# Conditioning vector spread by TensorE instead of by DMA, at the start of a one-core SSD and attention trunk

## Chip, cores and metric

The kernel runs on one core of one Trainium2 chip. The metric is the device time of one execution in microseconds (us). Three runs of the kernel before gave a median of 1242.96 us (1242.60 to 1243.46). Every quantity of time below is in us unless it says ns.

## The reference

Two layers, each with a modulation (shift, scale, gate) that is computed from one conditioning vector `c`. Sizes: 256 tokens, width 2048, all float32.

```python
def _adaln(c, w, b):
    mod = jax.nn.silu(c) @ w + b                 # c: (1, 2048), w: (2048, 6144)
    shift, scale, gate = jnp.split(mod, 3, axis=-1)
    return shift[:, None, :], scale[:, None, :], gate[:, None, :]

for layer in range(DEPTH):                       # DEPTH = 2
    shift, scale, gate = _adaln(c, ada_w[layer], ada_b[layer])
    h = x * (1.0 + scale) + shift
    y = _ssd_mixer(h, ...) if layer < N_A_LAYERS else _dilated_mixer(h, k_sh, v_sh, ...)
    x = _layer_norm(DEEPNORM_ALPHA * x + (1.0 + gate) * y, ln_g[layer], ln_b[layer])
    if layer == N_A_LAYERS - 1:
        k_sh, v_sh = _shared_kv(x, kv_w)
```

Layer 0 is a Mamba-2 (SSD) mixer: `h @ in_w` with 10304 output columns, a short convolution, a chunked scan, an output product. Layer 1 is a dilated window attention with keys and values shared from layer 0's output. Nearly all work is in the weight products.

## The kernel before, in words

**Precision.** Each float32 weight piece (128 x 1024 values, 512 KB, tile `raw`) is split in two fp32r parts: ScalarE copies it to `whi` (`split`, L99), VectorE writes the rest `raw - whi` to `wlo` (L101), and TensorE then makes three matmuls for each block: high by high, high by low, low by high (L150 to L152 for products with the weights as stationary operand, L212 to L214 for the other orientation). The activations `h`, kept transposed with 16 blocks `kt` of 128 channels in the tile `actT`, are split in the same way into `hhi` and `hlo`.

**The modulation.** Channel block `kt` of `h` needs two numbers per channel, `scale` and `shift`. Each is a dot product of a 2048-long row of `ada_w` with silu(c). The kernel holds silu(c) in all 128 partitions (tile `cb_`, 128 x 2048). A load of 1 MB brings 128 rows of `ada_w` (tile `araw`, L288), and one VectorE instruction multiplies them by `cb_` and sums along the row (`ada_dot`, L295, a SCALAR_TENSOR_TENSOR with an accumulated output into `mod`). So each of the 16 blocks costs two loads of 1 MB and two such dot products; 96 of them in the whole program.

**The start.** `c` (8 KB in memory) is loaded with a zero stride over partitions, so that one DMA of 1 MB writes the same row in all 128 partitions (`bcast`, L63 and L67), and ScalarE applies silu to 128 x 2048 in place (L68). Behind it on the same DMA queue (SyncE, SP, issues all loads) come two `araw`, the input block `xt`, the biases `adab`, the first weight piece, two more `araw`, and then more weight pieces. SP has eight semaphores for its DMAs and uses them in turn, so the ninth load, the second weight piece, is issued when the first load, `c`, has landed.

**The step of one block**, `h_step`, called twice for each `kt`: dot product for `scale`, dot product for `shift`, the addition of the biases (`ada_bias`, L300), then on ScalarE `htmp = x * scale + shift` (L463) and `hhi` (L465), then on VectorE `hlo` (L467). For blocks 0 and 1 the program is written out by hand: after block 0, two plain float32 products start from `htmp` without a split (`plain`, L503, four matmuls of 256 columns each, which the profile counts as eight), and only the second half of their weight pieces is split (`half`, L511 and L512) for block 1. From there a list of products (`order`) is worked through piece by piece, with `h_step` calls between them; partial sums of products that cannot be finished yet are put away from PSUM to SBUF by ScalarE (`put_away`, L568). A list scheduler of the framework decides the order on each engine within these constraints, and `tc.issue_after` pins some of them.

**PSUM.** The pool `mm` has four tiles of one bank, the pool `ex` has another four, which hold the first two products (`first`) through the whole phase.

The few lines of the start that the change touches:

```python
    cb_ = cons.tile([P, D], F32, name="cb_")
    bcast(cb_, c)
    S.activation(cb_, cb_, AF.Silu)
```

## Time and profile before

| what | value |
|---|---|
| median of three runs | 1242.96 us (1242.60 to 1243.46) |
| the profiled execution, its own time | 1243.02 us |
| its span, first to last instruction | 1241.2 us |
| TensorE (PE) busy | 1216.1 us, 98% of the span, 7078 matmuls |
| weight loads of TensorE (PEld) | 1043.9 us, 84% |
| VectorE (DVE) busy | 1028.3 us, 83% |
| ScalarE (ACT) busy | 702.4 us, 57% |
| DMA read from memory | 332.47 MB, mean 270 GB/s |
| DMA in the first 155 us (five slices of the page) | 384, 421, 423, 422, 421 GB/s |

The profiled execution took 1.8 us more than its span; that part lies around the instructions. It is 0.06 us over the median of the three runs. A line of the timeline gives the start and the duration in us, the engine, the line of the program, the operation, what it writes and reads, and how many equal instructions it merges; in brackets stands the engine's idle time before it and what ended it. Matmuls overlap in the records, so the distance between two starts, and not the duration, tells the pace.

### The profile page before, as it was taken

To read this page: it belongs to the slowest core of one execution; us is meant where nothing else is said; L and a number is where in the kernel's file an instruction comes from. 1 tells how busy PE (TensorE), PEld (TensorE's weight loads), DVE (VectorE), ACT (ScalarE), POOL (GpSimd) and SP (SyncE) were. 2 spreads that over 40 slices of the span, in tenths; PEclk is the share of its full clock that TensorE was granted. 3 is DMA by queue.
4 is the path that set the end of the run, shared out by engine and by line. 5 is a ranking of instruction groups with operands and counts; after the bars stand their busy time and mean duration, and the time that the engine had idled before them with its cause. 6 is when DMAs were issued, how large, how long until landed. Compare 5 with 4: busy or idle time off the path is not lost.

```text
span 1241.2 us, 18711 instructions
## 1 busy us (share of the span) xinstructions
PE 1216.1 (98%) x7078; PEld 1043.9 (84%) x7078; DVE 1028.3 (83%) x1454; ACT 702.4 (57%) x1045; POOL 0.2 (0%) x4
## 2 busy tenths in 40 slices
PE   4999999999999999999999999999999999999997
PEld 4989988898888888888888788888888888888886
DVE  5999986999988989899768678889978867658777
ACT  3555477868597789764345544434435644444631
POOL 0000000000000000000000000000000000000000
PEclk9999999999999999999999999999999999999999
DMA  9999977687656456699998569989997774463751
GB/s 384 421 423 422 421 270 245 226 295 257 213 193 208 166 172 202 214 338 346 356 320 293 192 199 381 353 340 368 380 375 294 229 263 132 136 205 118 233 175 68
DMA packets 80587, 335.88 MB, mean 271 GB/s; under 512 B 9105, under 2 KB 9329, under 8 KB 67697
## 3 DMA queue, kind: packets, MB, share of 16 engines
q1 hardware_dynamic: 80496, 334.69, 74.9%
q8 instruction: 55, 0.90, 0.3%
q14 instruction: 36, 0.29, 0.1%
HBM read 332.47 MB, written 2.18 MB: 270 GB/s over the span
## 4 chain that ended last, share of the span: by engine, by line
PE 83%; DMA 8%; DVE 6%; ACT 2%; issue 1%; DVEq 0%; ACTq 0%; SPq 0%
PE acc L181 24%; PE acc L184 12%; PE acc L213 12%; PE acc L214 12%; PE acc L212 11%; DMA raw<-in_win 6%; DVE wlo L101 2%; PE acc L150 2%; PE acc L152 2%; PE acc L151 2%; PE py L705 1%; DVE araw L295 1%; DMA araw<-in_ada 1%; ACT whi L99 1%; PE acc L915 1%
## 5 line engine op out<-in xcount | busy, mean ns | idle before, releaser
L99 ACT ACTIVATE whi<-raw 128x1024 fp32r<-128x1024 f32 x390 | 409.5, 1058 | 355.5 <-PE acc L214 137.5
L101 DVE TENSOR_TENSOR wlo<-raw,whi 128x1024 fp32r<-128x1024 f32 x390 | 470.3, 1221 | 142.9 <-ACT whi L99 138.4
L181 PE MATMUL acc<-actT,whi 128*128 128x512 f32 x1280 | 405.3, 397 | 0.0
L184 PEld LDWEIGHTS acc<-actT,wlo 128*128 128x128 f32 x1280 | 239.4, 188 | 55.6 <-DVE wlo L101 0.4
L213 PE MATMUL acc<-wlo,actT 128*128 128x512 f32 x656 | 257.1, 392 | 0.8 <-DVE wlo L101 0.8
L212 PE MATMUL acc<-whi,actT 128*128 128x512 f32 x656 | 253.3, 394 | 0.0
L184 PE MATMUL acc<-actT,wlo 128*128 128x256 f32 x1280 | 252.9, 279 | 0.0
L295 DVE SCALAR_TENSOR_TENSOR araw<-araw,cb__72 128x2048 f32<-128x2048 f32 x96 | 219.3, 2285 | 9.9 <-DMA araw<-in_ada 9.8
L181 PEld LDWEIGHTS acc<-actT,whi 128*128 128x128 f32 x1280 | 195.9, 189 | 0.4
L214 PE MATMUL acc<-whi,actT 128*128 128x512 f32 x432 | 169.0, 391 | 0.0
L213 PEld LDWEIGHTS acc<-wlo,actT 128*128 128x128 f32 x656 | 123.2, 188 | 27.2 <-DVE wlo L101 2.1
L212 PEld LDWEIGHTS acc<-whi,actT 128*128 128x128 f32 x656 | 122.7, 188 | 24.1
L150 PE MATMUL acc<-actT,whi 128*128 128x256 f32 x376 | 106.9, 286 | 0.0
L151 PE MATMUL acc<-actT,whi 128*128 128x256 f32 x376 | 106.1, 284 | 0.0
L152 PE MATMUL acc<-actT,wlo 128*128 128x256 f32 x376 | 104.6, 285 | 0.4 <-DVE wlo L101 0.4
L214 PEld LDWEIGHTS acc<-whi,actT 128*128 128x128 f32 x432 | 81.1, 188 | 16.7
L214 PE MATMUL acc<-whi,ylo 128*128 128x512 f32 x224 | 87.5, 391 | 0.0
L150 PEld LDWEIGHTS acc<-actT,whi 128*128 128x128 f32 x376 | 72.7, 193 | 0.6
L151 PEld LDWEIGHTS acc<-actT,whi 128*128 128x128 f32 x376 | 72.7, 193 | 0.4
L152 PEld LDWEIGHTS acc<-actT,wlo 128*128 128x128 f32 x376 | 71.5, 193 | 0.7 <-DVE wlo L101 0.6
L214 PEld LDWEIGHTS acc<-whi,ylo 128*128 128x128 f32 x224 | 42.1, 188 | 8.6
L663 ACT ACTIVATE seg<-cbc,cumT 128x128 f32<-128x128 f32 x128 | 41.0, 389 | 5.1 <-DVE wlo L101 2.3
(278 smaller groups left out, 1124.2 us busy)
## 6 DMA issues: line engine op xcount, KB each, us to landing
araw<-in_ada SPq DMA_DIRECT2D x96, 1024.0 KB, 7.4
raw<-in_win SPq DMA_DIRECT2D x112, 512.0 KB, 6.7
raw<-in_wout SPq DMA_DIRECT2D x64, 512.0 KB, 5.9
raw<-in_wbin SPq DMA_DIRECT2D x64, 512.0 KB, 4.2
raw<-in_wxs SPq DMA_DIRECT2D x48, 512.0 KB, 4.6
raw<-in_wv SPq DMA_DIRECT2D x48, 512.0 KB, 6.7
raw<-in_wk SPq DMA_DIRECT2D x48, 512.0 KB, 7.6
cbc<-cumd SPq DMA_DIRECT2D x16, 512.0 KB, 5.0
```

The costliest lines, as they stand in the source:

```text
L99: copied.append(S.activation(hi, raw, AF.Copy))
L101: latest.append(V.tensor_tensor(lo, raw, hi.bitcast(F32), op=ALU.subtract))
L150: T.matmul(o, hi[:, k, c_], ahi[:, kt, :], start=first, stop=False, skip_group_check=True)
L151: T.matmul(o, hi[:, k, c_], alo[:, kt, :], start=False, stop=False, skip_group_check=True)
L152: T.matmul(o, lo[:, k, c_], ahi[:, kt, :], start=False, stop=kt == k1 - 1, skip_group_check=True)
L181: T.matmul(ps[n], hi[:, k, n * P:n * P + P], both(kt), start=kt == 0, stop=False, skip_group_check=True)
L184: T.matmul(ps[n][:, 0, :], lo[:, k, n * P:n * P + P], high(kt), start=False, stop=kt == KT - 1, skip_group_check=True)
L212: T.matmul(o, h_, hi[:, k, :], start=kt == k0, stop=False, skip_group_check=part)
L213: T.matmul(o, h_, lo[:, k, :], start=False, stop=False, skip_group_check=part)
L214: end = T.matmul(o, l_, hi[:, k, :], start=False, stop=kt == k1 - 1, skip_group_check=part)
L295: return V.scalar_tensor_tensor(raw, raw, 1.0, cb_, op0=ALU.mult, op1=ALU.mult, accum_out=mod[layer][:, ct, j:j + 1])
L663: S.activation(seg[:, hh, b, :], cbc[:, hh, b, :], AF.Relu, bias=cumT[:, b, h0 + hh:h0 + hh + 1], scale=-1.0)
```

## The change

`c` is laid out by the host as 16 rows of 128 values, with a 16 x 16 identity beside it (16 x 144 values, 9 KB). One small DMA brings it to 16 partitions, into a corner of `cb_`, and silu is applied to 16 x 128. TensorE then makes, for each row `j`, one matmul whose stationary operand is column `j` of the identity repeated 128 times and whose moving operand is the 16 x 128 block: it writes row `j` to all 128 partitions of a PSUM tile `cps` (128 x 2048, four banks, in a pool that is closed before `ex` is opened). Six matmuls of a tile of ones with itself stand ahead of these sixteen. ScalarE copies the four banks to `cb_`. The two dot products of block 0 read `cps` instead of `cb_`; the first is made as two halves of 1024 with an addition behind them. The "+1" on two of the biases (L519) moves behind the second dot product in the program.

```diff
     cb_ = cons.tile([P, D], F32, name="cb_")
-    bcast(cb_, c)
-    S.activation(cb_, cb_, AF.Silu)
+    crow = cb_[:KT, :P + KT]
+    nc.sync.dma_start(crow, c)
+    S.activation(crow[:, :P], crow[:, :P], AF.Silu)
...
-                ex = c0.enter_context(tc.tile_pool(name="ex", bufs=4, space=PSUM))
-                first = [acc_pair(ex), acc_pair(ex)]
+                cE = ExitStack()
+                ec = cE.enter_context(tc.tile_pool(name="ec", bufs=1, space=PSUM))
+                cps = ec.tile([P, D], F32, name="cps")
+                warm = mm.tile([P, 2, L], F32, name="acc")[:, 0, :P]
+                for _ in range(6):
+                    T.matmul(warm, ones, ones, start=True, stop=True)
+                for j in range(KT):
+                    T.matmul(cps[:, j * P:j * P + P], crow[:, P + j:P + j + 1].to_broadcast([KT, P]), crow[:, :P],
+                             start=True, stop=True)
+                for n in range(4):
+                    S.activation(cb_[:, 512 * n:512 * n + 512], cps[:, 512 * n:512 * n + 512], AF.Copy)
...
-                    h_step.dot = ada_dot(0, kind, kt, raw)
+                    if not kt and kind == "scale":
+                        part0 = mod[0][:, 0, 2:3]
+                        V.scalar_tensor_tensor(raw[:, :D // 2], raw[:, :D // 2], 1.0, cps[:, :D // 2], op0=ALU.mult,
+                                               op1=ALU.mult, accum_out=part0)
+                        V.scalar_tensor_tensor(raw[:, D // 2:], raw[:, D // 2:], 1.0, cps[:, D // 2:], op0=ALU.mult,
+                                               op1=ALU.mult, accum_out=scale(0, 0))
+                        V.tensor_tensor(scale(0, 0), scale(0, 0), part0, op=ALU.add)
+                    else:
+                        h_step.dot = ada_dot(0, kind, kt, raw, cps if not kt else None)
...
                     if kind == "shift":
+                        if not kt:
+                            with tc.issue_after(h_step.dot.ins):
+                                V.tensor_scalar(adab[:, :, :, 1:3], adab[:, :, :, 1:3], 1.0, None, op0=ALU.add)
...
-                V.tensor_scalar(adab[:, :, :, 1:3], adab[:, :, :, 1:3], 1.0, None, op0=ALU.add)
...
+                cE.close()
+                ex = c0.enter_context(tc.tile_pool(name="ex", bufs=4, space=PSUM))
+                first = [acc_pair(ex), acc_pair(ex)]
+                pss[-2], pss[-1] = first
```

The order of the instructions moves at three places. `DMAHW0` to `DMAHW7` are the semaphores of SP's loads, `Activation` counts ScalarE's instructions, `PE` TensorE's, `DVE` VectorE's own.

On VectorE, from the first dot product to the split of the second weight piece, there stood before (`cb__72` is `cb_`, `mod_84` holds shift, scale and gate of layer 0):

```order
L295 SCALAR_TENSOR_TENSOR araw,mod_84<-araw,cb__72 128x2048 [waits DMAHW1_49,Activation_49]
L295 SCALAR_TENSOR_TENSOR araw,mod_84<-araw,cb__72 128x2048 [waits DMAHW2_49]
L519 TENSOR_SCALAR adab<-adab 128x32x2 [waits DMAHW4_49]
L300 TENSOR_TENSOR mod_84<-mod_84,adab 128x2 [waits DVE_49]
L467 TENSOR_TENSOR actT<-htmp,actT 128x256 [waits Activation_49]
L512 TENSOR_TENSOR wlo<-raw,whi 128x512 [waits DMAHW5_49,Activation_49]
L295 SCALAR_TENSOR_TENSOR araw,mod_84<-araw,cb__72 128x2048 [waits DMAHW6_49]
L295 SCALAR_TENSOR_TENSOR araw,mod_84<-araw,cb__72 128x2048 [waits DMAHW7_49]
L300 TENSOR_TENSOR mod_84<-mod_84,adab 128x2 [waits DVE_49]
L467 TENSOR_TENSOR actT<-htmp,actT 128x256 [waits Activation_49]
L512 TENSOR_TENSOR wlo<-raw,whi 128x512 [waits DMAHW0_49,Activation_49]
```

and now:

```order
L464 SCALAR_TENSOR_TENSOR araw,mod_84<-araw,cps 128x1024 [waits DMAHW1_49,PE_49,Activation_49]
L466 SCALAR_TENSOR_TENSOR araw,mod_84<-araw,cps 128x1024
L296 SCALAR_TENSOR_TENSOR araw,mod_84<-araw,cps 128x2048 [waits DMAHW2_49]
L468 TENSOR_TENSOR mod_84<-mod_84 128x1 [waits DVE_49]
L480 TENSOR_SCALAR adab<-adab 128x32x2 [waits DMAHW4_49]
L301 TENSOR_TENSOR mod_84<-mod_84,adab 128x2 [waits DVE_49]
L488 TENSOR_TENSOR actT<-htmp,actT 128x256 [waits Activation_49]
L296 SCALAR_TENSOR_TENSOR araw,mod_84<-araw,cb__72 128x2048 [waits DMAHW6_49,DMAHW0_49]
L533 TENSOR_TENSOR wlo<-raw,whi 128x512 [waits DMAHW5_49,Activation_49]
L296 SCALAR_TENSOR_TENSOR araw,mod_84<-araw,cb__72 128x2048 [waits DMAHW7_49]
L301 TENSOR_TENSOR mod_84<-mod_84,adab 128x2 [waits DVE_49]
L488 TENSOR_TENSOR actT<-htmp,actT 128x256 [waits Activation_49]
```

The first dot product has a wait on TensorE and on ScalarE where it had one on ScalarE; the addition of the two halves is new; and the third dot product (block 1, scale) now stands ahead of the half split of the first weight piece, which stood ahead of it.

In the built program the first half's wait on `PE` is for the count 22, six and sixteen matmuls, which TensorE raises once behind the sixth and once behind the sixteenth; its wait on `Activation` is for the count 5, the silu and four copies, and the four copies raise that count once, behind the fourth.

On ScalarE the program began before with:

```order
L68 ACT_TABLE_LOAD
L68 ACTIVATE cb__72<-cb__72 128x2048 [waits DMAHW0_49]
L463 ACTIVATE htmp<-xt,mod_84 128x256 [waits DMAHW3_49,DVE_49]
L465 ACTIVATE actT<-htmp 128x256 [waits Activation_49]
L511 ACTIVATE whi<-raw 128x512 [waits DMAHW5_49]
```

and begins now with:

```order
L69 ACT_TABLE_LOAD
L69 ACTIVATE cb__72<-cb__72 16x128 [waits DMAHW0_49]
L442 ACTIVATE cb__72<-cps 128x512 [waits PE_49,Activation_49]
L442 ACTIVATE cb__72<-cps 128x512 x3
L484 ACTIVATE htmp<-xt,mod_84 128x256 [waits DMAHW3_49,DVE_49]
L486 ACTIVATE actT<-htmp 128x256 [waits Activation_49]
```

The copies of the spread rows stand between the silu and block 0's `htmp`; the first of them waits for TensorE's count 22 too, since `cb_`'s corner is what the matmuls read.

A little later on ScalarE, from the split of the third weight piece on (`s_101`, `s_103` are the places where two partial sums are put away), there stood before:

```order
L99 ACTIVATE whi<-raw 128x1024 [waits DMAHW1_49]
L99 ACTIVATE whi<-raw 128x1024 [waits DMAHW2_49]
L568 ACTIVATE s_101<-acc 128x512 [waits PE_49]
L99 ACTIVATE whi<-raw 128x1024 [waits DMAHW3_49,PE_49]
L568 ACTIVATE s_101<-acc 128x512 [waits PE_49]
L568 ACTIVATE s_103<-acc 128x512 [waits PE_49] x2
L99 ACTIVATE whi<-raw 128x1024 [waits DMAHW4_49,DVE_49]
```

and now:

```order
L100 ACTIVATE whi<-raw 128x1024 [waits DMAHW1_49]
L592 ACTIVATE s_101<-acc 128x512 [waits PE_49] x2
L100 ACTIVATE whi<-raw 128x1024 [waits DMAHW2_49]
L592 ACTIVATE s_103<-acc 128x512 [waits PE_49] x2
L100 ACTIVATE whi<-raw 128x1024 [waits DMAHW3_49]
L100 ACTIVATE whi<-raw 128x1024 [waits DMAHW4_49,DVE_49]
```

Two put-aways moved ahead of the fourth piece's copy and two ahead of the fifth's. Behind these places the order of all engines is the one before.

More of the change, by code (lines that the diff above doesn't have):

```diff
@@ L289, in ada_load, with ada_dot @@
         return raw
-    def ada_dot(layer, kind, ct, raw):
+    def ada_dot(layer, kind, ct, raw, by=None):
         j = KIND.index(kind)
         with tc.issue_after(pin[0]) if pin[0] is not None else ExitStack():
-            return V.scalar_tensor_tensor(raw, raw, 1.0, cb_, op0=ALU.mult, op1=ALU.mult,
+            return V.scalar_tensor_tensor(raw, raw, 1.0, by if by is not None else cb_, op0=ALU.mult, op1=ALU.mult,
                                    accum_out=mod[layer][:, ct, j:j + 1])
@@ L487, in trunk @@
                 source = {"dt": wdt, -2: win[0], -1: win[4], **{n: p[0] for n, p in zip(names, begun.values())}}
-                pss = {-2: first[0], -1: first[1]}
+                pss = {}
                 pieces = []
@@ L1236, in _layout @@
     return {
-        "xT": x[0].T.reshape(KT, P, L).transpose(1, 0, 2), "x": x[0], "c": c, "par": par, "cst": cst, "bias": bias,
+        "xT": x[0].T.reshape(KT, P, L).transpose(1, 0, 2), "x": x[0], "c": np.concatenate([c.reshape(KT, P), np.eye(KT, dtype=f)], 1), "par": par, "cst": cst, "bias": bias,
         "lnrow": np.stack([ln_g[0], ln_b[0], ln_g[1], ln_b[1]]),
```

## Prediction

> **What bounds the kernel now.** The first view is the table of stretches: length of the stretch, busy time of TensorE (PE) with its number of matmuls, then weight loads, VectorE (DVE), ScalarE (ACT), GpSimd, granted clock, DMA share and GB/s.
>
> ```profile
> 14.00:25.00 11.00, 9.04 (x24) 7.04 (x25) 8.44 (x11) 4.53 (x8) 0.00 (x0) 1.00 1.03 425
> 25.00:160.00 135.00, 135.00 (x920) 125.86 (x919) 125.98 (x134) 72.55 (x95) 0.00 (x0) 1.00 1.02 420
> ```
>
> From 25 to 160 us TensorE is busy for all of 135.00 us, VectorE for 126 of them, and the DMA engines are full at 420 GB/s. Three resources run side by side; the one that never pauses is TensorE. Whatever the change does at the start, it can reach the end only by moving TensorE's work behind 25 us earlier or later. So the second view is TensorE's timeline up to there, for its pace (the distance of two starts).
>
> ```profile
> 14.02 3.78 PE L503 MATMUL acc<-htmp,raw 128*128 128x256 f32 x8 [14.02 <-ACT htmp L463]
> 19.74 3.78 PE L503 MATMUL acc<-htmp,raw 128*128 128x256 f32 x8 [1.94 <-DMA raw<-in_win]
> 25.23 0.41 PE L150 MATMUL acc<-actT,whi 128*128 128x256 f32 x1
> 25.45 0.35 PE L151 MATMUL acc<-actT,whi 128*128 128x256 f32 x1
> 25.63 0.28 PE L152 MATMUL acc<-actT,wlo 128*128 128x256 f32 x1
> 25.75 0.28 PE L150 MATMUL acc<-actT,whi 128*128 128x256 f32 x1
> ```
>
> TensorE starts at 14.02, waits from 17.80 to 19.74 for a weight piece, and then runs on. Up to 25.45 a fp32r matmul of 256 columns takes 0.21 to 0.22 us, behind 25.63 it takes 0.12: a slow pace and a fast one. The first run of 3.78 us stayed slow; the unbroken run from 19.74 turned fast 5.8 us after its start.
>
> The third view is VectorE's timeline from the first dot product (L295) to the split of the piece that TensorE needs next at 42 us. Of the rows between, those are left out that only repeat a kind.
>
> ```profile
> 8.36 2.29 DVE L295 SCALAR_TENSOR_TENSOR araw<-araw,cb__72 128x2048 f32<-128x2048 f32 x1 [7.36 <-DMA araw<-in_ada]
> 10.58 0.08 DVE L295 DVE_READ_ACCUMULATOR araw<-araw,cb__72 128x1 f32 x1
> ...
> 12.95 0.19 DVE L519 TENSOR_SCALAR adab<-adab 128x64 f32<-128x64 f32 x1
> 13.17 0.16 DVE L300 TENSOR_TENSOR mod<-mod,adab 128x2 f32<-128x2 f32 x1
> 14.44 0.42 DVE L467 TENSOR_TENSOR actT<-htmp,actT 128x256 fp32r<-128x256 f32 x1 [1.11 <-ACT actT L465]
> 14.96 0.69 DVE L512 TENSOR_TENSOR wlo<-raw,whi 128x512 fp32r<-128x512 f32 x1
> 15.97 2.29 DVE L295 SCALAR_TENSOR_TENSOR araw<-araw,cb__72 128x2048 f32<-128x2048 f32 x1 [0.32 <-DMA araw<-in_ada]
> 18.48 2.29 DVE L295 SCALAR_TENSOR_TENSOR araw<-araw,cb__72 128x2048 f32<-128x2048 f32 x1 [0.20 <-DMA araw<-in_ada]
> 20.81 0.16 DVE L300 TENSOR_TENSOR mod<-mod,adab 128x2 f32<-128x2 f32 x1
> 22.09 0.43 DVE L467 TENSOR_TENSOR actT<-htmp,actT 128x256 fp32r<-128x256 f32 x1 [1.12 <-ACT actT L465]
> 23.56 2.36 DVE L101 TENSOR_TENSOR wlo<-raw,whi 128x1024 fp32r<-128x1024 f32 x2 [0.25 <-ACT whi L99]
> 26.93 1.22 DVE L101 TENSOR_TENSOR wlo<-raw,whi 128x1024 fp32r<-128x1024 f32 x1 [1.01 <-ACT whi L99]
> 34.59 1.23 DVE L101 TENSOR_TENSOR wlo<-raw,whi 128x1024 fp32r<-128x1024 f32 x1 [0.69 <-ACT whi L99]
> 35.73 0.42 DVE L467 TENSOR_TENSOR actT<-htmp,actT 128x256 fp32r<-128x256 f32 x1
> 36.07 2.28 DVE L295 SCALAR_TENSOR_TENSOR araw<-araw,cb__72 128x2048 f32<-128x2048 f32 x1
> 38.28 0.08 DVE L295 DVE_READ_ACCUMULATOR araw<-araw,cb__72 128x1 f32 x1
> 40.61 0.16 DVE L300 TENSOR_TENSOR mod<-mod,adab 128x2 f32<-128x2 f32 x1
> 40.72 1.23 DVE L101 TENSOR_TENSOR wlo<-raw,whi 128x1024 fp32r<-128x1024 f32 x1
> ```
>
> At the end of this stretch the two engines touch:
>
> ```profile
> 41.80 0.28 PE L151 MATMUL acc<-actT,whi 128*128 128x256 f32 x1
> 42.00 0.39 PE L152 MATMUL acc<-actT,wlo 128*128 128x256 f32 x1
> ```
>
> The subtraction that starts at 40.72 ends at 41.95, and TensorE's matmul with its `wlo` starts at 42.00, 0.08 later than the pace of 0.12 would have it. Here TensorE has no reserve against VectorE: if VectorE's chain from its first dot product to this subtraction ends later, TensorE and all behind it are later by that much. That chain is what I sum.
>
> **The change, part by part.** *When the first dot product can start.* The wait that ended last before it was its own load (8.36); the silu was done before. In the new order it waits for all sixteen spreading matmuls and for all four copies, as the counts 22 and 5 say; the second half of the dot has no wait of its own. So cutting it into halves starts nothing early. I sum TensorE's time, then ScalarE's.
>
> ```profile
> 0.73 0.38 SPq L63 DMA_DIRECT2D cb__72<-in_c  x1
> 0.82 0.17 DVE L84 MEMSET ones<- 128x128 f32 x1 [0.82 <-PEq L1252]
> 1145.99 1.05 PE L1055 MATMUL po<-pT,b 128*128 128x128 f32 x8
> ```
>
> The warm-up matmuls can start when `ones` is written, at about 1.05. A plain fp32 matmul shows as two rows. Eight rows of 256 columns took 3.78; less the 0.20 by which a slow row outlasts its pace (0.41 against 0.21) that is 0.45 each, and 0.22 for 128 columns (estimate). Six matmuls are 12 rows: 2.6, to 3.65. Sixteen spreading matmuls are 32 rows. At the fast pace a row of 128 columns takes 0.11 (eight rows in 1.05, less 0.16 of tail). Bounds: 32 x 0.11 = 3.5 if all are fast, 32 x 0.22 = 7.0 if all are slow. Between them the pace turns where an unbroken run is between 3.8 us (did not turn) and 5.8 us (had turned) old; from 1.05 on that is 4.85 to 6.85. I take the middle, 5.85: 10 rows slow, 22 fast, 8.25; with 0.2 for the last result, 8.45. The ends give 8.0 and 9.0, no turn at all 10.85. No row has matmuls with 16 partitions; I price them by their columns, and keep "no turn" as a rival. [...]
>
> What could be later than the warm-up is `c` itself. Its 1 MB was there at 5.84 (below); the next megabyte took until 8.36, 2.5 more. So 9 KB land at the latest at 5.84 - 2.5 = 3.3, at the earliest soon behind the issue at 1.11; silu on 128 columns takes at most the 0.42 of a copy of 256. At most 3.7, hidden by the warm-up to within 0.1.
>
> ```profile
> 5.84 1.91 ACT L68 ACTIVATE cb__72<-cb__72 128x2048 f32<-128x2048 f32 x1 [3.83 <-DMA cb__72<-in_c]
> 13.37 0.60 ACT L463 ACTIVATE htmp<-xt,mod 128x256 f32<-128x256 f32 x1 [5.62 <-DVE mod L300]
> 14.00 0.42 ACT L465 ACTIVATE actT<-htmp 128x256 fp32r<-128x256 f32 x1
> 22.48 1.99 ACT L99 ACTIVATE whi<-raw 128x1024 fp32r<-128x1024 f32 x2
> 26.80 1.55 ACT L568 ACTIVATE s<-acc 128x512 f32<-128x512 f32 x3
> ```
>
> Four copies of 512 from PSUM: three take 1.55, four 2.1. With two hops of 0.05 the first dot product starts at 8.45 + 2.1 + 0.1 = **10.65** (10.2 to 11.2; 13.05 without a turn), against 8.36. Its load, 2.5 earlier, is there at 5.9 and is no longer what ends last. Behind the waiting dot on VectorE stand all further dots and splits; behind the copies on ScalarE stands only block 0's `htmp`, which needs the dots anyway. [...]
>
> *VectorE's chain behind it, first part* (to the subtraction at 22.09). Before: 22.09 - 8.36 = 13.73. Now, start to start: two halves at the 1.14 of an equally long subtraction, 2.28; a dot product 2.22 (8.36 to 10.58; reading PSUM is priced like SBUF); the addition 0.11 (40.61 to 40.72); biases +1, 0.22; bias and the way over ScalarE to the subtraction, 1.27; subtraction 0.34 (35.73 to 36.07); the third dot 2.21; half split 0.60 (between 0.34 and 1.14); the fourth dot 2.33 (38.28 to 40.61); bias and ScalarE 1.28. Sum 12.86, so 0.87 less than before: the waits for loads at 15.97 and 18.48 go, since the loads land 2.5 earlier, and the half split has its ScalarE copy ready.
>
> *Second part* (22.09 to 40.72, 18.63). The same instructions. Before, VectorE waited on ScalarE for 0.25 + 1.01 + 0.69 = 1.95. Now two put-aways stand ahead of each of two copies: each makes VectorE wait 2 x 0.52 (from 1.55 for three) plus a copy of 1.0, less its own subtraction of 1.14: 0.9, twice, and 0.3 for the first; 2.1 in all. So 18.78.
>
> Sum: 10.65 + 12.86 + 18.78 = 42.29 against 40.72, **1.6 us later**. TensorE itself is ready sooner: its first split matmuls follow the ScalarE copy of block 1, at about 23.4, and it is fast by then, as the plain products run unbroken from 16.7. Their first twelve took 2.8 before, up to 25.75; at 0.12 they end at 24.85, 0.9 ahead. So TensorE waits some 2.5 at the place where it had no reserve. *Free of cost:* the accumulator that the warm-up takes, one of four, reused behind TensorE's own work; `ex` opening late, as `cps` is last read at about 15; the "+1", still behind the two dots; the second weight piece, issued at once and 2.5 sooner, at 17.2, when TensorE is still in the first product; 1 MB less of DMA, which only gives the loads a longer lead.
>
> The profiled execution took 1243.02 (0.06 over the median); 1243.02 + 1.6 = **1244.6**.
>
> **The rivals.** *No turn of the pace* while 16 partitions are in use, or a break between warm-up and spread: the first dot at 13.05, all else equal, 4.0 later, 1247.0, slower. For: the run from 14.02 stayed slow for 3.78 us. Against: nothing distinguishes the rows but their partitions. It decides from a first dot at 11.55 on: there the delay passes 2.5 us.
>
> *The DMA lead decides.* The chain of waits in this phase names loads:
>
> ```profile
> 61.20 11.52 DMA raw<-in_win
> 72.80 11.69 DMA raw<-in_win
> ```
>
> If the stage to 155 us were set by the full queue, 1 MB less would end it 2.5 earlier: 1240.6. Against it stands TensorE's 135.00 of 135.00. The chain runs through loads because each was issued when a buffer came free, 11.5 us before; that is a queue's length, not a shortage.
>
> *The halves work as named*, so that the first starts behind eight matmuls and beside the copies: about 6.7, and the sum is 2.0 to 2.5 earlier than before, 1240.5 to 1241.0. Against it stand the counts 22 and 5.
>
> **How the numbers follow.** The forecast has 0.62, no turn 0.20, the DMA lead 0.06, working halves 0.07, 0.05 something not listed. The forecast's own range is a first dot at 10.2 to 11.2, +1.1 to +2.1, and with 0.4 for runs among themselves 1243.7 to 1245.5. The range reaches up over the no-turn case and down below the time before: 1242.6 to 1247.3. A measurement of this kernel tells about 0.2%, 2.5 us, from no change. Slower by more has the no-turn case and 0.12 of the forecast's upper end, 0.32; faster by more, half of the two early cases, 0.06; within it, 0.62.
>
> **What would show it.** The first dot product between 10.2 and 11.2, straight behind the fourth copy, with its load long landed; no gap between warm-up and spread, and the pace turning within the spread; TensorE's longest wait behind 25 us at a `wlo` matmul near 43.5; from there the same work as before at a constant distance. I am wrong if the first dot starts before the last copy ends, if TensorE's start and not VectorE's chain sets the distance, or if the distance shrinks behind 50 us.

## The result, and the profile after

The changed kernel takes 1247.57 us (median of 18 executions, 1243.03 to 1250.50) against 1243.06 for the kernel before (18 executions, 1242.60 to 1244.53). The ratio is 1.0030, 95% interval 1.0023 to 1.0037: 3.7 us slower, 2.9 to 4.6. That is the distance of the means (1246.9 and 1243.2); the medians lie 4.5 apart. Two more measurements, below, gave 1.0026 and 1.0027. I had forecast +1.6 and a range of 1242.6 to 1247.3; the median lies 0.3 above that range, the time before plus 3.7 within it. My rival "no turn of the pace" had +4.0.

The median is not the time of any one kind of execution. Each execution lists its mean granted TensorE clock, and by it the 39 executions of the changed kernel, from the three measurements, fall into three groups (65 executions of the kernel before beside them: median 1243.13):

| mean granted clock | executions | time, median (range) |
|---|---|---|
| 0.993 to 0.995 | 10 | 1243.80 (1243.03 to 1245.01) |
| 0.999 to 1.000 | 16 | 1247.02 (1245.73 to 1248.18) |
| 0.997 to 0.998 | 13 | 1248.23 (1247.14 to 1250.50) |

The profile that came with the result is of the first group (1243.79, span 1242.0). Its table of stretches, with the columns as in the prediction:

```profile
14.00:25.00 11.00, 8.45 (x30) 6.70 (x31) 8.35 (x15) 4.49 (x8) 0.00 (x0) 0.65 1.02 421
25.00:160.00 135.00, 133.27 (x907) 124.05 (x906) 126.55 (x135) 71.83 (x96) 0.00 (x0) 1.00 1.01 416
```

TensorE now lacks 1.73 of its 135.00, where before it lacked nothing. Its clock column has 0.65 between 14 and 25: by the trace's records the granted clock was 1.00 from 4.62 to 8.04, 0.50 from there to 21.69, and 1.00 again behind it. The timeline of the start, TensorE, then ScalarE, then VectorE, and the place behind 40 us:

```profile
1.04 2.93 PE L437 MATMUL acc<-ones 128*128 128x128 f32 x12 [1.04 <-DVE ones L85]
3.90 4.16 PE L439 MATMUL cps<-cb__72 16*128 16x128 f32 x32
```

```profile
8.16 2.06 ACT L442 ACTIVATE cb__72<-cps 128x512 f32<-128x512 f32 x4 [5.42 <-PE cps L439]
```

```profile
10.26 1.22 DVE L464 SCALAR_TENSOR_TENSOR araw<-araw,cps 128x1024 f32<-128x1024 f32 x1 [9.26 <-ACT cb__72 L442]
...
41.65 1.22 DVE L102 TENSOR_TENSOR wlo<-raw,whi 128x1024 fp32r<-128x1024 f32 x1
```

```profile
42.93 0.39 PE L153 MATMUL acc<-actT,wlo 128*128 128x256 f32 x1 [1.73 <-DVE wlo L102]
```

Twelve warm-up rows, straight behind them 32 rows of the spread in 4.16 us (0.13 each on average, so most of them fast), four copies, the first dot product at 10.26, and at 41.65 the subtraction that stood at 40.72 before. TensorE waits 1.73 for it. The chain is the one I summed; in this execution it is 0.93 late at that place.

The last experiment brought a profile of the same kernel in an execution of the third group (1247.78, span 1246.0). The same places:

```profile
1.04 2.93 PE L437 MATMUL acc<-ones 128*128 128x128 f32 x12 [1.04 <-DVE ones L85]
3.90 7.19 PE L439 MATMUL cps<-cb__72 16*128 16x128 f32 x32
...
45.98 0.38 PE L153 MATMUL acc<-actT,wlo 128*128 128x256 f32 x1 [1.73 <-DVE wlo L102]
...
47.36 0.41 PE L153 MATMUL acc<-actT,wlo 128*128 128x256 f32 x1
47.58 0.41 PE L151 MATMUL acc<-actT,whi 128*128 128x256 f32 x1
```

```profile
13.29 1.22 DVE L464 SCALAR_TENSOR_TENSOR araw<-araw,cps 128x1024 f32<-128x1024 f32 x1 [12.29 <-ACT cb__72 L442]
...
44.70 1.23 DVE L102 TENSOR_TENSOR wlo<-raw,whi 128x1024 fp32r<-128x1024 f32 x1
...
136.08 1.41 DVE L590 TENSOR_TENSOR s<-acc,s 128x512 f32<-128x512 f32 x2 [0.75 <-PE acc L153]
...
160.27 1.22 DVE L102 TENSOR_TENSOR wlo<-raw,whi 128x1024 fp32r<-128x1024 f32 x1
```

The spread takes 7.19, so all of its rows are at the slow pace, 0.22. The first dot product starts at 13.29, the subtraction at 44.70, 3.98 later than before. Then something comes that the first profile doesn't have: behind its wait, from 47.15 to 50.56, TensorE runs at the slow pace again (16 rows 0.21 apart instead of 0.12, a loss of 1.5). At 136.08 VectorE waits 0.75 for an accumulator of TensorE. For a while TensorE, not VectorE, is the late one.

**Where the time comes from.** I take one VectorE instruction near the end of the stage, the subtraction that starts at 155.97 before, as a mark. It starts 0.14 later in the first profile and 4.30 later in the second. What follows the mark takes 1085.3 before, and 1085.9 and 1085.7 in these two. Over all fourteen profiles of this study it is 1084.2 to 1087.1, whatever the kernel's start was, so a single total carries about 1 us of chance from there. I compare kernels at the mark, and totals only as medians.

Between 41 and 155 us the distance does not stay constant, as I had said it would. It shrinks by 0.8 in both profiles, nearly all of it at three VectorE instructions between 96 and 107 us. The kernel before, and the changed one in the first profile, at the first of them and at the mark:

```profile
96.39 2.29 DVE L295 SCALAR_TENSOR_TENSOR araw<-araw,cb__72 128x2048 f32<-128x2048 f32 x1 [0.27 <-DMA araw<-in_ada]
...
155.97 1.22 DVE L101 TENSOR_TENSOR wlo<-raw,whi 128x1024 fp32r<-128x1024 f32 x1
```

```profile
96.92 2.29 DVE L296 SCALAR_TENSOR_TENSOR araw<-araw,cb__72 128x2048 f32<-128x2048 f32 x1
...
156.11 1.22 DVE L102 TENSOR_TENSOR wlo<-raw,whi 128x1024 fp32r<-128x1024 f32 x1
```

Before, VectorE waits 0.27 there for a load, and 0.08 and 0.07 at two instructions behind it; each wait also costs the 0.08 by which neighbouring rows overlap otherwise. After, it is later, and all three waits are gone. By 107 us the distance has fallen from 0.93 to 0.15. For the first wait the view names the load; the second comes straight behind a ScalarE copy that had waited 0.24 for a load; the third it doesn't name. So the loads were a second bound, close behind VectorE's chain. With the mark the account of the second profile closes: 3.98 at the subtraction, 3.21 behind the loads, 3.35 before VectorE's wait for TensorE, 4.30 behind it. The other 0.46 of its 4.76 lie behind the mark, in what is chance from profile to profile.

### The profile page after: what moved, and what is told of

It reads as the page before. It is cut to its first block, busy times and chain, and to the rows that moved or that the text cites. A ratio compares the mean times of both kernels' runs of the same rounds, so it can differ in the third digit from the quotient of the medians.

```text
span 1242.0 us, 18810 instructions
## 1 busy us (share of the span) xinstructions
PE 1221.3 (98%) x7122; PEld 1049.3 (84%) x7122; DVE 1027.8 (83%) x1457; ACT 701.5 (56%) x1049; POOL 0.2 (0%) x4
## 4 chain that ended last, share of the span: by engine, by line
PE 88%; DVE 7%; ACT 2%; DMA 2%; issue 1%; DVEq 0%; SPq 0%; ACTq 0%
PE acc L182 24%; PE acc L185 12%; PE acc L214 12%; PE acc L215 12%; PE acc L213 12%; PE acc L151 3%; PE acc L153 3%; PE acc L152 3%; DVE araw L296 2%; DVE wlo L102 1%; PE py L729 1%; ACT whi L100 1%; DMA raw<-in_wv 1%; PE acc L939 1%; PE aux L1053 1%
## 5 line engine op out<-in xcount | busy, mean ns | idle before, releaser
L296 DVE SCALAR_TENSOR_TENSOR araw<-araw,cb__72 128x2048 f32<-128x2048 f32 x94 | 214.8, 2285 | 0.4 <-DMA araw<-in_ada 0.4
```

Of the source, the lines that this page charges most:

```text
L296: return V.scalar_tensor_tensor(raw, raw, 1.0, by if by is not None else cb_, op0=ALU.mult, op1=ALU.mult, accum_out=mod[layer][:, ct, j:j ...
```

## The experiments

Each kernel stands beside the kernel before on the same chip. Times are medians, in brackets the 95% interval of the ratio. The columns "second dot", "subtraction" and "mark" are starts on VectorE in the profile: the dot product behind the first one (10.73 before), the subtraction at 40.72 before, and the mark at 155.97 before.

| kernel | us (before) | ratio | second dot | subtraction | mark, against before |
|---|---|---|---|---|---|
| changed (result's profile) | 1247.57 (1243.06) | 1.0030 [1.0023, 1.0037] | 12.55 | 41.65 | +0.14 |
| changed, again | 1246.69 (1243.22) | 1.0026 [1.0017, 1.0035] | 12.56 | 41.66 | +0.14 |
| changed, third | 1247.02 (1243.12) | 1.0027 [1.0016, 1.0037] | 15.58 | 44.70 | +4.30 |
| spread on 128 rows | 1243.78 (1243.22) | 1.0007 [0.9998, 1.0016] | 12.61 | 41.72 | +0.21 |
| that, with a load behind `c` | 1244.88 (1243.55) | 1.0016 [1.0007, 1.0025] | 12.82 | 42.11 | +0.60 |
| no warm-up | 1244.70 (1243.22) | 1.0014 [1.0005, 1.0023] | 14.41 | 43.32 | +1.80 |
| warm-up on 16 rows | 1246.44 (1243.55) | 1.0026 [1.0015, 1.0036] | 15.29 | 44.38 | +2.85 |
| ten warm-ups | 1247.10 (1243.43) | 1.0030 [1.0019, 1.0042] | 17.29 | 46.41 | +6.02 |
| per bank | 1244.90 (1243.55) | 1.0015 [1.0006, 1.0024] | 12.91 | 42.22 | +0.70 |
| per bank, no warm-up | 1242.64 (1243.43) | 0.9996 [0.9987, 1.0005] | 11.82 | 40.93 | -0.59 |
| fp32r, 4 x 512 | 1242.11 (1243.55) | 0.9989 [0.9981, 0.9998] | 9.55 | 38.85 | -1.40 |
| fp32r, again | 1242.22 (1243.12) | 0.9994 [0.9985, 1.0002] | 9.59 | 39.88 | -1.43 |
| fp32r, with a load behind `c` | 1243.91 (1243.43) | 1.0001 [0.9992, 1.0010] | 11.28 | 40.53 | +0.70 |

From the second dot product to the subtraction twelve of these thirteen profiles take 28.9 to 29.3, whatever came before. In the second fp32r profile (30.29) TensorE waited 1.93 for a weight piece, its granted clock between 14 and 25 us was 0.84 (1.00 in the first fp32r profile), and ScalarE's put-away waited for it; the kernel before (29.99) waited for loads and has another order there. So in these profiles the whole change acts through one number, the start of that dot product; and between the subtraction and the mark 0.8 is given back, unless loads or a fallen clock come in.

**The changed kernel again.**

> The changed kernel as it is, to see one of its longer executions. Theory A (TensorE's pace does not turn fast during the spread in most executions, since matmuls on 16 partitions do not keep the clock released): the profile shows 32 rows of the spread at 0.21 us, ending near 10.9, the first dot product near 13.1, and the time 1246.5 to 1248.5; a few executions, in which the turn falls into the spread, stay at 1243 to 1244. Theory B (the start is always as in the first profile, first dot at 10.3, and the longer executions lose their time later in the program): the spread ends near 8.1 and an idle stretch of 3 to 5 us stands somewhere behind 45 us. On theory A alone I reach about 1246.8, so a part of 1 us of the median of 1247.57 is not explained yet.

1246.69 against 1243.22, so the slowdown is no matter of one chip. Three of the 11 executions had a clock of 0.993 or 0.994 and took 1243.80 to 1244.57, the other eight 1245.88 to 1248.91. The profile was again one of the short ones (second dot at 12.56). What follows: there are two kinds of executions, and the mean clock tells them apart. What makes the longer ones long this run doesn't show, since none of them was profiled.

**Spread on 128 rows.** The host pads the 16 rows with zeros, so that the matmuls contract over 128 partitions; columns, number and place stay.

```diff
-    crow = cb_[:KT, :P + KT]
+    crow = cb_[:, :P + KT]
...
-                    T.matmul(cps[:, j * P:j * P + P], crow[:, P + j:P + j + 1].to_broadcast([KT, P]), crow[:, :P],
+                    T.matmul(cps[:, j * P:j * P + P], crow[:, P + j:P + j + 1].to_broadcast([P, P]), crow[:, :P],
```

> The same sixteen spreading matmuls, but over 128 partitions: rows 16 to 127 of c and of the identity are zeros, so the result is the same, and the load is 74 KB instead of 9 KB. Theory A: with all partitions in use the run from 1.05 on is unbroken work, the pace turns fast at the latest 7.9 us into the program in every execution, the spread ends between 7.7 and 9.4, and all executions lie at 1243 to 1245. Theory A' (zeros or few values in the array count as no activity, not the number of partitions): no difference from the kernel after, median 1247 to 1248. Theory B: no difference either.

1243.78, and all eleven executions had a clock of 0.995 to 0.997 and took at most 1246.20. I read that as an early turn in every one of them; the profile shows it for one, with a granted clock of 0.92 in the first 14 us and a spread that ends at 8.12. The 7.9 by which the turn was to come was an estimate of mine that no run shows. The spread:

```profile
3.77 4.35 PE L439 MATMUL cps<-cb__72 128*128 128x128 f32 x32
```

What follows: with the same instructions in the same place, the spread took 4.35 on 128 partitions, with a clock of 0.995 to 0.997 in all 11 executions; on 16 it took 4.16 in the first profile and 7.19 in the long one, and 10 executions of 39 had a clock of 0.993 to 0.995. The rows added are zeros, so it isn't the values. This takes back 2.9 us of the 3.5 by which the changed kernel was slower on that chip.

**No warm-up.** The six matmuls of `ones` are left out.

```diff
-                for _ in range(6):
-                    T.matmul(warm, ones, ones, start=True, stop=True)
```

> Without the six warm-up matmuls. Theory A: the spread starts at 2.8 instead of 3.9, runs slow throughout in every execution and ends at 9.8 instead of 10.95, so the first dot product comes at about 12.0; all executions lie close together at about 1.1 us below the long executions of the kernel after, 1245.5 to 1247, and none at 1243. Theory C (the warm-up does what it is named for, and the spread keeps it going): the spread is slower without it than with it in most executions and the median is above the kernel after.

1244.70, 2.0 faster than with them on the same chip, and 0.8 below the lower end of what I had expected. No execution turned early (clocks 0.999 to 1.000). In the profile the spread ran slow throughout, but it started at 2.74 instead of 3.90. TensorE's spread and VectorE's first dot product:

```profile
2.74 7.19 PE L436 MATMUL cps<-cb__72 16*128 16x128 f32 x32 [2.74 <-ACT cb__72 L69]
```

```profile
12.12 1.22 DVE L461 SCALAR_TENSOR_TENSOR araw<-araw,cps 128x1024 f32<-128x1024 f32 x1 [11.13 <-ACT cb__72 L439]
```

What follows: ahead of a spread on 16 partitions the warm-ups cost more, by the 1.16 by which they delay it, than they gain in the one execution of four in which they turn the pace. The 1.16 is not all of the 2.0: the long profile above loses 1.5 at the slow pace from 47.15 to 50.56, as other executions with warm-ups may, and about 0.7 stays unexplained (last experiment).

**Warm-up on 16 rows.**

```diff
-                    T.matmul(warm, ones, ones, start=True, stop=True)
+                    T.matmul(warm, ones[:KT], ones[:KT], start=True, stop=True)
```

> The six warm-up matmuls use 16 of the 128 partitions of the tile of ones; number, columns and place stay. Theory A (matmuls on 16 partitions never bring TensorE to its fast pace; in the changed kernel only the warm-up does, in about one execution of four): no execution has a granted clock of 0.993 or 0.994, all have 0.997 or more; the profile shows the spread of 32 rows at 0.21 to 0.22 each, 6.9 us from 3.9 on, the first dot product at about 13.0, and the median lies at 1247 to 1248. Theory B (partitions do not matter, the phase of the clock does): the profile is that of the changed kernel (spread 4.2 us, first dot at 10.3, clock 0.994), about a quarter of the executions are short ones, and the median is 1246.7.

TensorE's warm-up and spread, then VectorE's first dot product:

```profile
1.04 2.92 PE L437 MATMUL acc<-ones 16*128 16x128 f32 x12 [1.04 <-DVE ones L85]
3.77 7.03 PE L439 MATMUL cps<-cb__72 16*128 16x128 f32 x32
```

```profile
13.00 1.22 DVE L464 SCALAR_TENSOR_TENSOR araw<-araw,cps 128x1024 f32<-128x1024 f32 x1 [12.00 <-ACT cb__72 L442]
```

44 rows without a gap, ten us of them, and no turn: theory A. Six of the seven executions had a clock of 0.999 or 1.000; one showed 0.949 without being longer (1246.85), and I have no trace of it. The median, 1246.44, is 0.6 under what I had expected, since I had not yet found the 0.8 that the loads give back: +2.85 at the mark is +2.9 in the time.

**Per bank.** The rows of `c` go to another tile (`cc`, loaded later), `cps` becomes four tiles of a bank, each bank is copied behind its own four matmuls, and the dot products read the copy.

```diff
+    crow = cc[:KT, :P + KT]
...
-                cps = ec.tile([P, D], F32, name="cps")
+                cps = [ec.tile([P, 512], F32, name=f"cps{n}") for n in range(4)]
...
-                for n in range(4):
-                    S.activation(cb_[:, 512 * n:512 * n + 512], cps[:, 512 * n:512 * n + 512], AF.Copy)
+                    if j % 4 == 3:
+                        S.activation(cb_[:, 128 * j - 384:128 * j + 128], cps[j // 4], AF.Copy)
```

> The 16 rows of c lie in another tile than the one that the copies write, the PSUM tile is four tiles of a bank each, each bank is copied behind its own four matmuls, and the first dot products read the copy. Warm-ups stay. Theory C (the halves gain nothing because one tile for all four banks makes the copies wait for all 16 matmuls and the dot for all four copies): copies run beside the matmuls, the first half dot starts 0.1 behind the second copy (about 6.6 in an execution with the early turn), the second half behind the fourth (about 8.6), so the end of the first dot product lies 2.7 earlier than in the changed kernel, in the profile and in every kind of execution: median 1244.0, short executions 1241.2. Rival (something else holds the first dot product back, or the stage behind it absorbs the gain): within 0.5 us of the changed kernel's 1246.7.

ScalarE's second copy and VectorE's two halves, in an execution without the early turn:

```profile
7.72 0.60 ACT L442 ACTIVATE cb__72<-cps 128x512 f32<-128x512 f32 x1 [1.11 <-PE cps L439]
```

```profile
8.35 1.23 DVE L464 SCALAR_TENSOR_TENSOR araw<-araw,cb__72 128x1024 f32<-128x1024 f32 x1 [7.35 <-ACT cb__72 L442]
...
11.76 1.23 DVE L466 SCALAR_TENSOR_TENSOR araw<-araw,cb__72 128x1024 f32<-128x1024 f32 x1 [2.18 <-ACT cb__72 L442]
```

The first half starts behind the second copy, while TensorE still spreads, and the second dot product comes 2.67 earlier than in the long profile of the changed kernel (12.91 against 15.58). The time is 1.35 over the kernel before, where the changed kernel's three medians are 3.5 to 4.5 over: 2.1 to 3.2 less, around the 2.7; the rival (within 0.5) is out. The median is 0.9 above the 1244.0 that I had expected, and the one execution with an early turn (clock 0.993) took 1243.68, not 1241.2. What follows: the wait for all sixteen matmuls and all four copies came from the tiles, and cutting the dot product into halves gains only where the tiles are cut too. Which of the three cuts (another tile for `c`, a tile per bank, dots that read the copy) is needed the run doesn't separate.

**Per bank, no warm-up**: both edits together.

> The per-bank kernel without its six warm-up matmuls, spread still with plain matmuls on 16 rows. The spread starts with silu's end at 2.75 instead of 3.90, all slow, a bank each 1.78; fourth copy done at 10.4, second half of the first dot at 10.5 (11.76 with warm-ups). Theory (what counts is when the first dot product ends, and the stage gives back 0.8 of any delay up to 155 us): the dot ends 0.4 later than before, the time is 0.4 under the kernel before to equal. Rival (the warm-ups bring something besides the spread's pace, for instance an earlier turn behind it): no better than with warm-ups, 1244.9 against 1243.5.

VectorE's second half:

```profile
10.67 1.23 DVE L463 SCALAR_TENSOR_TENSOR araw<-araw,cb__72 128x1024 f32<-128x1024 f32 x1 [2.18 <-ACT cb__72 L439]
```

1242.64 against 1243.43; the interval of the ratio covers 1, so the total doesn't tell it from the kernel before. The mark is 0.59 earlier than before. With warm-ups the distance was +1.35, so the rival is out.

**fp32r, 4 x 512.** Tiles as in the per-bank kernel; `c` as 4 rows of 512, split in a high and a low part, two fp32r matmuls a bank.

```diff
...
+                S.activation(chi, crow, AF.Copy)
+                V.tensor_tensor(clo[:, :512], crow[:, :512], chi[:, :512].bitcast(F32), op=ALU.subtract)
+                for n in range(4):
+                    for part, c4 in enumerate((chi, clo)):
+                        T.matmul(cps[n], chi[:, 512 + n:513 + n].to_broadcast([4, P]), c4[:, :512],
+                                 start=not part, stop=bool(part))
+                    S.activation(cb_[:, 512 * n:512 * n + 512], cps[n], AF.Copy)
```

> As the per-bank kernel, but c comes as 4 rows of 512 with a 4 x 4 identity, is split into a high and a low fp32r part (ScalarE copy, VectorE subtraction), and each bank gets two fp32r matmuls of 512 columns instead of four plain ones of 128; no warm-ups. At the slow pace a row of 512 fp32r columns should take 0.42, eight rows 3.4 us, from about 3.6 to 7.2; first half dot at about 6.0, second at about 7.7. Theory (the end of the whole program follows VectorE's chain, one us for one us, also when it is earlier than before): 2.4 us less than the kernel before, 1240.8. Rival (the start of TensorE or the loads bind as soon as VectorE's chain is earlier): no better than the kernel before, 1243.2 or above, with TensorE or VectorE waiting for a load between 14 and 50 us.

1242.11 against 1243.55, 1.4 less where I had expected 2.4. Half of the missing 1.0 is lost ahead of 40 us: the second half of the dot started at 8.40 instead of 7.7, and VectorE's chain is 1.87 earlier at the subtraction (38.85), not 2.4. The other half is lost behind it, where ScalarE waits longer for weight pieces than before (7.0 between 25 and 50 us, against 4.2). Its waits there (line, what for, us in total, times, longest):

```profile
ACT whi L100 <- DMA raw<-in_win: 7.0, 3, 3.5
```

The third of these waits, before and now, and the VectorE subtraction that is held up in turn:

```profile
43.77 1.06 ACT L99 ACTIVATE whi<-raw 128x1024 fp32r<-128x1024 f32 x1 [0.96 <-DMA raw<-in_win]
```

```profile
42.93 1.06 ACT L100 ACTIVATE whi<-raw 128x1024 fp32r<-128x1024 f32 x1 [1.99 <-DMA raw<-in_win]
```

```profile
45.94 1.23 DVE L102 TENSOR_TENSOR wlo<-raw,whi 128x1024 fp32r<-128x1024 f32 x1 [0.39 <-ACT whi L100]
```

The piece is there 0.84 earlier than before, not 1.87, and at 45.94 the distance falls from 1.86 to 1.39. TensorE's granted clock between 25 and 50 us was 0.93 here (1.00 before). The one wait near it that the view puts down to TensorE (0.38, at 49.95) stands also in the second fp32r profile (0.37), where the granted clock of that stretch was 1.00, and it is made up by 51.64. What follows: with the chain out of the way the loads bind, and what is left at the mark is 1.40. The second measurement (below) finds 1.43 there, though its subtraction stood at 39.88.

**A load behind `c`**, 0.92 MB, which puts back nearly the megabyte that the change takes out; once in the kernel with the spread on 128 rows, once in the fp32r kernel.

```diff
     nc.sync.dma_start(crow, c)
+    nc.sync.dma_start(cb_[:, 256:], ada[0, 2, 0][:, 256:])
```

> The kernel with c on 128 partitions (the spread on 128 rows), with one load more of 0.92 MB right behind c, into the part of the tile that the copies overwrite later. It puts back nearly all of the megabyte that the change takes out. Theory (the lead of the loads is worth nothing): the same time as without it, 1243.8, up to 0.3 more, the first dot product still behind the copies at 10.3. Rival (the full queue sets the end of the stage up to 155 us): 0.92 MB at 400 GB/s are 2.3 us, 1246.1.

> The fp32r kernel with the load of 0.92 MB right behind c put back, as in the run on 128 rows, where it moved VectorE by nothing that the first dot product had not. Theory (loads come second: they bind only where VectorE's chain is earlier than before; in the fp32r kernel ScalarE waits 1.5, 3.5 and 2.0 us for weight pieces at 31, 37 and 43 us): here the load costs 1 to 2.3 us, and the time comes back to the kernel before, within 0.5. Rival (what keeps the fp32r kernel from its full gain is only the fall of TensorE's clock at 41 us): the same as without the load, 1.4 under the kernel before.

On 128 rows the first dot product still waits for the copies,

```profile
10.53 1.22 DVE L465 SCALAR_TENSOR_TENSOR araw<-araw,cps 128x1024 f32<-128x1024 f32 x1 [9.53 <-ACT cb__72 L443]
```

0.21 later than without the load, and the mark is 0.39 later; the rival's 2.3 is not there. The medians are 0.8 apart in their distance to before, more than the 0.3 that I had allowed, but their intervals overlap and leave it unclear. In the fp32r kernel the load costs 2.10 at the mark and 1.4 to 1.9 in the distance to before: the first dot product waits for its own rows,

```profile
8.78 1.23 DVE L465 SCALAR_TENSOR_TENSOR araw<-araw,cb__72 128x1024 f32<-128x1024 f32 x1 [4.45 <-DMA araw<-in_ada]
```

and all the gain is gone. So the rival, that only the fall of the clock keeps the fp32r kernel from its full gain, is out. What follows: the lead of the loads is worth little, 0.4 at the mark, while the first dot product is as late as in the changed kernel's first profile, and up to 2 us once it isn't.

**Ten warm-ups.**

```diff
-                for _ in range(6):
+                for _ in range(10):
                     T.matmul(warm, ones, ones, start=True, stop=True)
```

> Ten warm-up matmuls instead of six. [...] The spread starts 1.6 later, at about 5.5, so an execution that hits has its first dot product at 10.5 to 11.5, one that does not at 14.7: median 1244 to 1245. Rival B (whether the pace turns has nothing to do with the length of the warm-up): a quarter of the executions with the low mean clock, and a median near 1248.

Three of six executions had a clock of 0.992 to 0.994 (1244.83 to 1246.86), three of 0.998 or more (1247.34 to 1249.29). An execution that "hits" is one of the first kind. Half of them did, more than the quarter of the rival, and six executions can't tell. The expected median of 1244 to 1245 took it that most would, which was my estimate and is not shown; 1247.10 missed it. The profile was one without a turn, with 4.64 us of warm-up:

```profile
1.05 4.64 PE L437 MATMUL acc<-ones 128*128 128x128 f32 x20 [1.05 <-DVE ones L85]
5.61 7.19 PE L439 MATMUL cps<-cb__72 16*128 16x128 f32 x32
```

In the two short profiles of the changed kernel 2.93 us of warm-up stand ahead of a spread of 4.16 and 4.17, in its long one and in the per-bank profile the same 2.93 ahead of 7.19, and here 4.64 ahead of 7.19. So a longer warm-up doesn't by itself bring the fast pace. What decides, beside the partitions, no run here shows.

**fp32r and the changed kernel, on one chip.**

> The fp32r kernel once more, on one chip with the changed kernel. If its gain is that of the profile at 155 us (1.4 us earlier than before), the ratio is 0.9989 again, with an interval that excludes 1; if the first result was scatter between executions, the interval covers 1.

> The changed kernel once more, on the same chip. Theory: two kinds of executions. Where the warm-up turns the pace (clock 0.993 or 0.994, about a quarter) the time is 0.5 to 1 over the kernel before; in the others the profile with 16-row warm-ups gives 2.9 at 155 us, so 2.9 over the kernel before, and 1.5 more in those with a clock of 0.998 or less, where TensorE's longer wait near 45 us costs it a window of half clock. Rival: no kinds, one spread of times around 2.5 over the kernel before, unrelated to the clock.

fp32r: 0.9994 [0.9985, 1.0002] this time, which covers 1. The profile has the same 1.43 at the mark, so I hold the gain for real, but that is argued from the traces: the totals of half a thousandth and one thousandth don't settle its size. Against the changed kernel it is 4.8 us faster on that chip (1242.22 against 1247.02). The changed kernel: three executions with a clock of 0.994 or 0.995 (median 1243.78), three of 0.999 or more (1247.00), four of 0.998 (1248.07). The kinds are there, and the step between the last two is 1.1. The middle kind is 3.9 over the kernel before where the mark of the 16-row kernel had given 2.9. Of that 1 us 0.3 is the later first dot product (13.29 against 13.00); the other 0.7 I can't explain, and no execution of the middle kind was profiled.

## Why the prediction was right or wrong

VectorE's chain held almost to the digit. What it starts from did not: the turn of TensorE's pace inside the spread failed to come in 29 of 39 executions, and these followed the rival "no turn of the pace", to which I gave 0.20. Against the kernel before, the three groups lie at +0.7, +3.9 and +5.1, so +1.6 describes none of them, and where a mean or a median over them falls, near the upper end of my range, is chance.

- **What bounds the kernel.** Right: VectorE's chain from the first dot product on sets the distance. The subtraction follows the second dot product by 28.9 to 29.3 in twelve profiles of thirteen. That TensorE has "no reserve" there was right too.
- **Warm-up and `c`.** Predicted 1.05 to 3.65 and `c` at most at 3.3: measured 1.04 to 3.90, and the silu at 2.4 to 2.5 with 0.31. Right, and it shows that the cover was not free: the spread could have started at 2.74.
- **End of the spread, 8.45: the step that failed.** I let the pace turn at 5.85, the middle of what one unbroken run of 128-partition matmuls had shown, and took the 16-partition matmuls as part of the same run. In the profile on record the granted clock was 1.00 from 4.62 on and the spread ended at 8.06; in three executions of four the turn does not come, and the end is 11.09. "Nothing distinguishes the rows but their partitions" was my reason against the rival, and the partitions were it. With 12 rows of warm-up ahead of it in both, the spread took 4.35 on 128 partitions and 7.19 on 16 in the long profile. Where inside a run the pace turns, no run here shows beyond these cases.
- **Copies and the first dot product.** 2.1 for four copies: 2.06. First dot product at 10.65, or 13.05 without a turn: 10.26 and 13.29, both straight behind the fourth copy. The halves gain nothing, as said; the per-bank run shows why.
- **The chain.** First part 12.86: 12.83 (10.26 to 23.09, the subtraction behind block 1). Second part 18.78: 18.56. With the first dot product as measured my two parts give +1.2, and +4.2 without a turn; measured at the subtraction are +0.93 and +3.98.
- **TensorE.** First split matmuls at 23.4: 23.11 in the first profile; its wait at a `wlo` matmul 1.73 instead of 2.5. In the long profile its start moves along (26.14), and the wait is 1.73 again. Not foreseen: behind it the long profile has TensorE at the slow pace from 47.15 to 50.56, 0.95 at the mark. Behind the same 1.73 the first profile stays fast (rows 0.12 apart from 43.15 on), so that the wait is the cause is not shown. The executions with a clock of 0.997 or 0.998 are 1.2 longer in the median than those with 0.999 or more. In the kernel before they are not longer (25 executions with 0.998 on four chips: median 1243.24; 35 with 1.000: 1243.17), so a lower mean clock alone doesn't make an execution longer; where in the program the slow stretch lies may matter, which no run here tests.
- **"A constant distance from there".** Wrong by 0.8, and by my own sign, a distance that shrinks behind 50 us. So even where the pace turned, the mark is +0.14 and not +1.6: 0.4 less by the earlier first dot product, 0.3 less by the chain, 0.8 given back to the loads. The rest of that group's +0.7 lies behind the mark. I had read VectorE's waits for loads up to 41 us only. Those at 96 to 107 us went the same way, since a chain that comes later finds its loads there. For the same reason my 0.06 for the lead of the loads fits this kernel and would be too low for a quicker one.

## What to carry to other kernels

A wait that is taken away uncovers the next one: before trading a transfer for engine work, list what is second at the place (here copies that wait for a whole tile) and price it at the engine's slow pace (here 7.19 for a spread of 32 rows, 4.16 at its fastest), unless a trace shows the fast one at that place. Cut the tiles where the consumer is cut, or the halves wait for the whole. Compare kernels at a mark behind the stage that was changed: with 1 us of chance in the 1085 us behind it, a total tells little, and a median over two kinds of executions hides both.

## What the runs showed of the hardware

- With a spread that contracts over 16 partitions its 32 rows took 7.19 in the long profile of the changed kernel, without warm-up and with ten warm-ups; in the kernel with the 16-row warm-up all 44 rows in a row were at 0.22 (10 us). With the spread on 128 partitions, 112 of them zeros, the 32 rows took 4.35, and the mean clocks of 0.995 to 0.997 speak for an early turn in all 11 executions. In the first profile of the changed kernel the granted clock was 1.00 from 4.62 to 8.04 and 0.50 from there, though the spread had kept TensorE busy up to 8.06.
- A wait of TensorE of 1.73 us was followed by rows at the slow pace in the long profile of the changed kernel (0.21 apart from 47.15 to 50.56), and in its first profile it was not (0.12 apart from 43.15 on). The granted clock between 25 and 50 us was 0.96 with ten warm-ups and 0.93 in the first fp32r profile, but 1.00 without warm-up and with the 16-row warm-up; between 14 and 25 us it was 0.84 in the second fp32r profile. What lowers it there stays open.
- The clock column can read 1.00 where the rows are slow. The first stretch of the kernel with the 16-row warm-up, in which all 44 rows were slow:

```profile
0.00:14.00 14.00, 9.75 (x44) 9.46 (x44) 1.18 (x3) 3.65 (x6) 0.20 (x4) 1.00 0.83 313
```

  The distance of the rows is to be trusted there, not the column.
